# Input squares taken as tiles land, later blocks' squares from token rows, and input scalings placed later in the passage

## The chip, the cores and the metric

The kernel runs on one core of a Trainium2 chip. The metric is the device time of one execution in microseconds (us). The engines are PE (TensorE, the matrix engine; PEld is its loading of weights), DVE (VectorE), ACT (ScalarE), POOL (GpSimd) and SP (SyncE, which here only issues DMAs). Each engine runs its own instructions in the order in which they were placed, and waits on semaphores for what other engines or DMAs deliver.

## The reference, cut to what matters

The reference is one inference step of a two-layer decoder trunk. Layer 0 is a Mamba-2 mixer and a SwiGLU feed-forward, layer 1 a sliding-window attention and a SwiGLU feed-forward. Of it, the change touches only the first step, the RMS norm of the input ahead of the mixer's input projection:

```
def _rmsnorm(x, g):
    xf = x.astype(jnp.float32)
    r = lax.rsqrt(jnp.mean(xf * xf, axis=-1, keepdims=True) + EPS)
    return (xf * r).astype(x.dtype) * g

zxbcdt = _rmsnorm(h, p['ssm_norm_g'][i]) @ w_in
...
dt_raw = zxbcdt[..., D_INNER + CONV_DIM:]
```

There are 64 sampled tokens, 16 meta tokens and 1024 prompt tokens, 1104 in all, each with 1024 features.

## The kernel before, in words

The 1104 tokens are worked on in two halves, of 592 and 512 tokens. A half's tokens lie in SBUF turned: features on the 128 partitions, as 8 tiles (`k`, KD = 8) of one column per token. A product in float32 precision is made of three matmuls on high and low parts: `uH` and `uL` of the activations, `wH` and `wL` of the weights. The high part is a cast on ACT, the low part a subtraction on DVE or POOL (`_split_high`, `_split_low`, `split_copy`).

Because the tokens stand on columns, their squares are summed over partitions by matmuls whose weights are a tile of squares (one block of up to 128 tokens) and whose moving operand is one column of ones. The mean goes from PSUM into `v` (DVE), the root is a power of -0.5 on POOL, and to scale columns the roots `r` are put on a diagonal (`dg`, DVE) and spread over all partitions by a matmul with ones. The first half has five blocks: three in its first part (336 tokens, `As`) and two in its second part (256 tokens, `Bs`).

`input_first` (the first 46 us) has an order written out by hand for PE, DVE, ACT and POOL (`in_order` adds dependencies between an engine's instructions in the order in which they were traced). It loads the tokens as two arrays, warms PE up with matmuls on ones, squares the first part two tiles at a time, sums, makes the roots, then scales and splits tile by tile and multiplies with the first two weight tiles (`dense`). In between it squares the second part on ACT and POOL, sums it on PE ahead of tile 6, and splits the low part of the weights on POOL. Then it scales and multiplies the second part. After it comes the convolution of the two finished products (`conv`, whose copies of `cstate` run on POOL), and the projection of dt.

`input_second` is the same norm for the second half, 512 tokens in four blocks. It is a generator whose steps `boundary` (the passage from the first half to the second) interleaves with the end of the first half by a string of letters: `x`, `s` and `b` are its steps (squares; sums, roots and diagonals; spread, scalings and splits), `l` the late gate of the last head group, `n`, `r`, `y` the steps of that group's norm, each `o` one product of the group before with `w_out`, each `w` one product of the last group. This string fixes the order of PE alone. A product accumulates in one of two accumulators (`acc`), which DVE frees by adding it to the residual (line 921).

All other order is that of a planner, which places instructions by its own simulated clock and by priorities (`ahead` raises them). It also orders the DMAs on SP's queue. Weights come through a ring of two raw tiles (`ws`), two high and two low tiles, and each split pair is also stored to DRAM (`kept`) for the second half.

Of the kernel before, what the change touches and what calls it, by code (L numbers as in the profile page):

```python
# [14 lines left out]
AF = mybir.ActivationFunctionType  # L15
ALU = mybir.AluOpType
# [4 lines left out]
D = 1024  # L21
KD = 8
# [4 lines left out]
EPS = 1e-5  # L27
# [67 lines left out]
class Weights:  # L95
# [67 lines left out]
    def load(self):  # L163
        for s in self.queue[: max(NWS - 1, 1)]:
            self._load(s)
# [82 lines left out]
class Mamba:  # L248
# [51 lines left out]
    def input_first(self):  # L300
# [7 lines left out]
        for q, k in ((nc.sync, 0), (nc.scalar, 4), (nc.sync, 2), (nc.scalar, 6)):  # L308
            load(q, 0, slice(k, k + 2))
        W._load(W.queue[0])  # L310
        load_vectors(K, I, self.hp)
        K.load_ident()
        W._load(W.queue[1])
        for k in (0, 4):
            load(nc.sync, 1, slice(k, k + 4))
        self.wdt = self.kp.tile([128, KD, 32], F32, name="wdt")
# [19 lines left out]
        def square(i, k, eng):  # L336
            d, src = sq[k // 4][:, k % 4 : k % 4 + 2, at[i]], h[:, k : k + 2, at[i]]
            if eng is nc.scalar:
                eng.activation(d, src, AF.Square)
            else:  # L340
                eng.tensor_tensor(d, src, src, ALU.mult)

        def sums(i, cs, order):
            ps = {c: self.ps() for c in cs}
            for x, k in enumerate(order):
                for c in cs:
                    o, n = blocks[c]
                    src = sq[k // 4][:, k % 4, o : o + n]
                    nc.tensor.matmul(ps[c][:n, 0:1], src, one[:, 0:1], start=x == 0, stop=x == KD - 1)
            return ps  # L350

        def means(ps, cs):
            for c in ps:
                n = blocks[c][1]
                nc.vector.tensor_scalar(v[:n, c : c + 1], ps[c][:n, 0:1], 1.0 / D, EPS, ALU.mult, ALU.add)
            nc.gpsimd.tensor_tensor(r[:, cs], v[:, cs], e[:, cs], ALU.pow)
# [32 lines left out]
        warm(5)  # L389
        for k, eng in ((0, nc.scalar), (4, nc.vector), (2, nc.scalar), (6, nc.vector)):  # L390
            square(0, k, eng)
        pa = sums(0, As, (0, 1, 4, 5, 2, 3, 6, 7))
        means(pa, A)
# [5 lines left out]
        W._split_low(W.queue[0], nc.gpsimd)  # L399
        scaled(0, 0, ra)  # L400
        for k in range(KD):
            high(0, k)
            if k + 1 < KD:
                scaled(0, k + 1, ra)
            low(0, k)
            if k in (4, 5):
                square(1, 2 * (k - 4), nc.scalar)
                square(1, 2 * (k - 4) + 4, nc.gpsimd)
            if k == 6:
                pb = sums(1, Bs, (0, 1, 4, 5, 2, 3, 6, 7))  # L410
                means(pb, B)
                W._split_low(W.queue[1], nc.gpsimd)
            for t in range(2):
                dense(t, 0, k, 0, self.uH, start=k == 0)
                dense(t, 0, k, 0, self.uL)
        diagonal(Bs)
        for t in range(2):
            for k in range(KD):
                dense(t, 0, k, 1, self.uH, stop=k == KD - 1)
            if t == 0:  # L420
                rb = spread(1, Bs)
                scaled(1, 0, rb)
        for k in range(KD):
            high(1, k)
            if k + 1 < KD:
                scaled(1, k + 1, rb)
            low(1, k)
            for t in range(2):
                dense(t, 1, k, 0, self.uH, start=k == 0)
                dense(t, 1, k, 0, self.uL)  # L430
                dense(t, 1, k, 1, self.uH, stop=k == KD - 1)
        for _ in range(2):
            W.queue.pop(0)
# [8 lines left out]
    def input_second(self):  # L442
# [6 lines left out]
        pair = [sq[:, 2 * i : 2 * i + 2, :n] for i in range(2)]  # L449
        for i in range(4):  # L450
            nc.scalar.activation(pair[i > 0], h[:, 2 * i : 2 * i + 2], AF.Square)
            if i:
                nc.gpsimd.tensor_tensor(pair[0], pair[0], pair[1], ALU.add)
        nc.gpsimd.tensor_tensor(sq[:, 0, :n], sq[:, 0, :n], sq[:, 1, :n], ALU.add)
        yield
        ps = self.ps()
        for c, (o, m) in enumerate(H["blocks"]):
            nc.tensor.matmul(ps[:m, 2 * c : 2 * c + 1], sq[:, 0, o : o + m], K.ones[:, 0:1], start=True, stop=True)
        v = self.small([128, 4], "xv")
        nc.vector.tensor_scalar(v[:], ps[:, :8].rearrange("p (c two) -> p c two", two=2)[:, :, 0], 1.0 / D, EPS, ALU.mult, ALU.add)  # L460
# [530 lines left out]
    def boundary(self, inp, G2, G):  # L991
# [6 lines left out]
        part = dict(x=inp, s=inp, b=inp, l=late, n=nrm, r=nrm, y=nrm, o=self.out(G2, 0), w=self.out(G, 0, True))  # L998
        for x in "xloosonoboorooywwwwwwww":
            next(part[x])  # L1000
# [38 lines left out]
    def run(self):  # L1039
        tc, nc, K, I, O = self.tc, self.nc, self.K, self.I, self.O  # L1040
        with ExitStack() as st:
# [16 lines left out]
            for hf in range(2):  # L1058
# [5 lines left out]
                if hf == 0:  # L1064
                    K.scratch = big[:, :4096]
                    self.input_first()
                    xbc = self.xbc(hf, 0, range(6))
                    next(xbc)
                    self.dt_proj(hf)
# [1598 lines left out]
def tokens(inputs):  # L2668
# [3 lines left out]
    return {"tokens_a": turned(x[:cut]), "tokens_b": turned(x[cut:end]), "tokens_c": turned(x[end:])}  # L2672
# [25 lines left out]
```

## Time and profile before

| | us |
|---|---|
| median of 3 runs | 2812.53 (2809.44 to 2813.52) |
| the profiled execution's own time | 2812.34 |
| its span in the trace | 2810.5 |
| PE busy | 2737.9 (97% of the span) |
| DVE busy | 1988.0 (71%) |
| ACT busy | 1196.4 (43%) |
| POOL busy | 541.6 (19%) |

Times in the profile are microseconds from the span's start. A row of the view of instructions in order of time gives the start, the duration, the engine, the line of the kernel, the operation, what it writes and reads, how many instructions were merged, and in brackets how long the engine had been idle before it and what ended that. A row of a view of stretches gives the stretch, its length, the busy time and number of instructions of each engine, the clock that TensorE was granted (1.00 is full), the DMA engines' busy share and GB/s. SPq, POOLq and so on are an engine's sequencer, which issues DMAs and waits.

### The profile page before, as it was taken

The page shows a single profiled execution, that of the slowest core. Times are in us where ns is not written, and L with a number is a line of the kernel's source. Part 1 is how long each engine was busy: PE and PEld are TensorE (multiplying, and loading weights), DVE is VectorE, ACT ScalarE, POOL GpSimd, SP SyncE. Part 2 cuts the span into 40 slices and gives each one's busy share as a digit, 9 for nine tenths or more (in the row PEclk, how much of TensorE's full clock was granted, in tenths as well). Part 3 has the DMA queues.
Part 4 walks back from the last instruction along what each step waited for, and adds up shares of the span by engine and source line. Part 5 has one row for each costly group of instructions (what it writes and reads, how often), then busy time and mean ns, then how long its engine had stood idle before and what let it go on. Part 6 is the DMA issues. An engine that isn't in the chain of part 4 may idle for free. (4 is left out here: it accounts for less than half of the span.)

```text
span 2810.5 us, 50267 instructions
## 1 busy us (share of the span) xinstructions
PE 2737.9 (97%) x19693; PEld 2532.9 (90%) x19693; DVE 1988.0 (71%) x3398; ACT 1196.4 (43%) x2483; POOL 541.6 (19%) x749
## 2 busy tenths in 40 slices
PE   8999999899999999999999999999999999999998
PEld 7888999887887799999999997767999999999998
DVE  5778666557574698787779791455479877877886
ACT  3666554347442244343343243456334433434224
POOL 2475545415233100000000002343220000000000
PEclk8999999999999899999999999999999999999999
DMA  6776766466554434344378662011714443447764
GB/s 218 242 241 203 268 224 232 174 235 208 198 179 163 146 101 175 123 161 142 127 262 310 240 211 90 23 30 36 225 59 140 157 141 125 164 141 285 276 219 160
DMA packets 260849, 495.45 MB, mean 176 GB/s; under 512 B 23556, under 2 KB 139908, under 8 KB 260612
## 3 DMA queue, kind: packets, MB, share of 16 engines
q1 hardware_dynamic: 256612, 485.00, 50.3%
q10 hardware_dynamic: 4000, 7.24, 0.7%
q8 instruction: 155, 2.54, 0.4%
q14 instruction: 82, 0.67, 0.1%
HBM read 316.87 MB, written 175.30 MB: 175 GB/s over the span
## 5 line engine op out<-in xcount | busy, mean ns | idle before, releaser
L1246 ACT CAST wo<-ws 128x512 fp32r<-128x512 f32 x428 | 264.5, 622 | 538.2 <-PE wacc L1591 250.9
L1590 PE MATMUL dacc<-bo,wo 128*128 128x276 f32 (+1 forms) x1232 | 355.6, 289 | 4.4 <-ACT sumX L1778 2.1
L1591 PE MATMUL dacc<-bo,wo 128*128 128x276 f32 (+1 forms) x1232 | 356.1, 289 | 0.0
L1592 PE MATMUL dacc<-bo,wo 128*128 128x276 f32 (+1 forms) x1232 | 354.9, 288 | 0.0
L1247 DVE TENSOR_TENSOR wo<-ws,wo 128x512 fp32r<-128x512 f32 x428 | 296.4, 697 | 55.4 <-ACT wo L1246 42.1
L75 PE MATMUL acc<-uH,wH 128*128 128x336 f32 (+2 forms) x808 | 269.0, 333 | 3.9 <-ACT wH L138 3.5
L77 PE MATMUL acc<-uH,wL 128*128 128x336 f32 (+2 forms) x808 | 267.7, 331 | 0.6 <-DVE wL L149 0.6
L76 PE MATMUL acc<-uL,wH 128*128 128x336 f32 (+2 forms) x808 | 268.2, 332 | 0.0
L1590 PEld LDWEIGHTS dacc<-bo,wo 128*128 128x128 f32 x1232 | 232.8, 189 | 5.2 <-ACT sumX L1778 2.3
L1591 PEld LDWEIGHTS dacc<-bo,wo 128*128 128x128 f32 x1232 | 231.8, 188 | 0.0
L1592 PEld LDWEIGHTS dacc<-bo,wo 128*128 128x128 f32 x1232 | 231.8, 188 | 0.0
L75 PEld LDWEIGHTS acc<-uH,wH 128*128 128x128 f32 x808 | 155.1, 192 | 20.3 <-issue 6.1
L76 PEld LDWEIGHTS acc<-uL,wH 128*128 128x128 f32 x808 | 154.9, 192 | 12.8 <-issue 4.1
L77 PEld LDWEIGHTS acc<-uH,wL 128*128 128x128 f32 x808 | 154.5, 191 | 12.8 <-issue 3.1
L668 DVE SCALAR_TENSOR_TENSOR cc<-raw,vectors_sb,cc 128x616 f32<-128x616 f32 (+1 forms) x144 | 133.9, 937 | 41.9 <-ACT cc L666 40.2
L2443 POOL MEMSET mask<- 128x64 f32 x1 | 0.2, 152 | 715.5 <-PE dacc L1592 715.5
L75 PE MATMUL acc<-yH,wH 128*128 128x336 f32 (+1 forms) x360 | 123.4, 343 | 5.8 <-DVE hA L921 3.0
L76 PE MATMUL acc<-yL,wH 128*128 128x336 f32 (+1 forms) x360 | 121.3, 337 | 0.5 <-DVE yL L82 0.5
L77 PE MATMUL acc<-yH,wL 128*128 128x336 f32 (+1 forms) x360 | 121.4, 337 | 0.2 <-DMA wL<-kept 0.2
L1766 DVE TENSOR_TENSOR hN<-hN,dacc 128x552 f32<-128x552 f32 (+1 forms) x132 | 95.0, 723 | 20.6 <-PE dacc L1592 19.9
L1590 PE MATMUL wacc<-B11H,wo 128*128 128x276 f32 (+1 forms) x352 | 105.4, 299 | 3.5 <-DVE big L921 3.5
L1590 PE MATMUL wacc<-N4H,wo 128*128 128x276 f32 (+1 forms) x352 | 102.3, 291 | 4.4 <-DVE hA L1603 1.9
(569 smaller groups left out, 8562.2 us busy)
## 6 DMA issues: line engine op xcount, KB each, us to landing
kept<-wH SPq DMA_DIRECT2D x56, 512.0 KB, 3.1
kept<-wL SPq DMA_DIRECT2D x56, 512.0 KB, 3.0
ws<-ffn_w_gate SPq DMA_DIRECT2D x44, 512.0 KB, 4.2
ws<-ffn_w_up SPq DMA_DIRECT2D x44, 512.0 KB, 4.9
ws<-ffn_w_down SPq DMA_DIRECT2D x44, 512.0 KB, 6.1
ws<-ssm_w_in SPq DMA_DIRECT2D x40, 512.0 KB, 6.5
wH<-kept SPq DMA_DIRECT2D x38, 512.0 KB, 3.4
wL<-kept SPq DMA_DIRECT2D x38, 512.0 KB, 4.3
```

The costliest lines, as they stand in the source:

```text
L75: nc.tensor.matmul(out, wH, xH, start=start, stop=False)
L76: nc.tensor.matmul(out, wH, xL, start=False, stop=False)
L77: nc.tensor.matmul(out, wL, xH, start=False, stop=stop)
L668: nc.vector.scalar_tensor_tensor(o, raw[:, k : k + n], w(k), o, ALU.mult, ALU.add)
L1246: nc.scalar.copy(H, src)
L1247: (low or nc.vector).tensor_tensor(L, src, H.bitcast(F32), ALU.subtract)
L1590: nc.tensor.matmul(out, wH, xH, start=start, stop=False, skip_group_check=True)
L1591: nc.tensor.matmul(out, wH, xL, start=False, stop=False, skip_group_check=True)
L1592: nc.tensor.matmul(out, wL, xH, start=False, stop=stop, skip_group_check=True)
L1766: add = lambda d, s: nc.vector.tensor_tensor(d, d, s, ALU.add)
L2443: nc.gpsimd.memset(A.mask0[:, :NS], NEG)
```

## The change

In `input_first`, one token load moves from ACT's queue to SP's, the second weight tile is loaded ahead of the small vectors, and two loads of token rows (tokens on partitions, 128x1024 each) are added into the tiles `rows`. Warm-up is three matmuls instead of five. The first part's squares are made one tile at a time, on ACT and DVE in turn, and each is summed at once. The later two blocks' squares are two ACT instructions on the rows with an accumulated sum per partition, which is a sum per token, so their matmuls leave PE. Scaling runs two tiles ahead instead of one. The low parts of the two weight tiles are split on DVE behind the first part instead of on POOL. The first convolution block's POOL instructions are ordered behind the last root. In `input_second`, the squares also come from four row loads, with accumulated sums on ACT; the additions on POOL and the sums on PE go. In `boundary`, the step with spread, scalings and splits stands behind two of the last group's products, and the norm's first two steps each stand one product earlier.

```diff
--- before.py
+++ after.py
@@ -305,14 +305,17 @@
         x = [I["tokens_a"], I["tokens_b"]]
         at = [slice(0, cut), slice(cut, H["n"])]
         load = lambda q, i, ks: q.dma_start(h[:, ks, at[i]], x[i][:, ks])
-        for q, k in ((nc.sync, 0), (nc.scalar, 4), (nc.sync, 2), (nc.scalar, 6)):
+        for q, k in ((nc.sync, 0), (nc.scalar, 4), (nc.sync, 2), (nc.sync, 6)):
             load(q, 0, slice(k, k + 2))
-        W._load(W.queue[0])
+        for w in W.queue[:2]:
+            W._load(w)
         load_vectors(K, I, self.hp)
         K.load_ident()
-        W._load(W.queue[1])
         for k in (0, 4):
             load(nc.sync, 1, slice(k, k + 4))
+        rows = [self.quad("xr") for _ in range(2)]
+        for i in range(2):
+            nc.sync.dma_start(rows[i][:], I["token_rows"][i])
         self.wdt = self.kp.tile([128, KD, 32], F32, name="wdt")
         nc.sync.dma_start(self.wdt[:].rearrange("p k m -> p (k m)"), I["ssm_w_in"][40, :, :256])
         load_params(K, I, self.kp)
@@ -333,26 +336,23 @@
             for _ in range(n):
                 nc.tensor.matmul(idle[:], one[:, :128], one[:, :512], start=True, stop=True)
 
-        def square(i, k, eng):
-            d, src = sq[k // 4][:, k % 4 : k % 4 + 2, at[i]], h[:, k : k + 2, at[i]]
-            if eng is nc.scalar:
-                eng.activation(d, src, AF.Square)
-            else:
-                eng.tensor_tensor(d, src, src, ALU.mult)
-
-        def sums(i, cs, order):
+        def sums(cs):
             ps = {c: self.ps() for c in cs}
-            for x, k in enumerate(order):
+            for x, (k, eng) in enumerate(product((0, 4, 2, 6), (nc.scalar, nc.vector))):
+                k += eng is nc.vector
+                d, src = tile(k, 0), h[:, k, at[0]]
+                if eng is nc.scalar:
+                    eng.activation(d, src, AF.Square)
+                else:
+                    eng.tensor_tensor(d, src, src, ALU.mult)
                 for c in cs:
                     o, n = blocks[c]
-                    src = sq[k // 4][:, k % 4, o : o + n]
-                    nc.tensor.matmul(ps[c][:n, 0:1], src, one[:, 0:1], start=x == 0, stop=x == KD - 1)
-            return ps
-
-        def means(ps, cs):
-            for c in ps:
+                    nc.tensor.matmul(ps[c][:n, 0:1], tile(k, 0)[:, o : o + n], one[:, 0:1], start=x == 0, stop=x == KD - 1)
+            for c in cs:
                 n = blocks[c][1]
                 nc.vector.tensor_scalar(v[:n, c : c + 1], ps[c][:n, 0:1], 1.0 / D, EPS, ALU.mult, ALU.add)
+
+        def roots(cs):
             nc.gpsimd.tensor_tensor(r[:, cs], v[:, cs], e[:, cs], ALU.pow)
 
         def diagonal(cs):
@@ -386,49 +386,50 @@
 
         A, B = slice(0, 3), slice(3, 5)
         As, Bs = range(0, 3), range(3, 5)
-        warm(5)
-        for k, eng in ((0, nc.scalar), (4, nc.vector), (2, nc.scalar), (6, nc.vector)):
-            square(0, k, eng)
-        pa = sums(0, As, (0, 1, 4, 5, 2, 3, 6, 7))
-        means(pa, A)
+        warm(3)
+        sums(As)
+        roots(A)
         diagonal(As)
         warm(1)
         ra = spread(0, As)
         for t in range(2):
             ws[t] = W._split_high(W.queue[t])
-        W._split_low(W.queue[0], nc.gpsimd)
-        scaled(0, 0, ra)
+        for k in range(2):
+            scaled(0, k, ra)
         for k in range(KD):
             high(0, k)
-            if k + 1 < KD:
-                scaled(0, k + 1, ra)
+            if k in (2, 4):
+                c = 2 + k // 2
+                nc.scalar.activation(rows[c - 3][:], rows[c - 3][:], AF.Square, accum_out=v[:, c : c + 1])
+            if k + 2 < KD:
+                scaled(0, k + 2, ra)
             low(0, k)
-            if k in (4, 5):
-                square(1, 2 * (k - 4), nc.scalar)
-                square(1, 2 * (k - 4) + 4, nc.gpsimd)
-            if k == 6:
-                pb = sums(1, Bs, (0, 1, 4, 5, 2, 3, 6, 7))
-                means(pb, B)
-                W._split_low(W.queue[1], nc.gpsimd)
+            if k == 5:
+                nc.vector.tensor_scalar(v[:, B], v[:, B], 1.0 / D, EPS, ALU.mult, ALU.add)
+                roots(B)
             for t in range(2):
                 dense(t, 0, k, 0, self.uH, start=k == 0)
                 dense(t, 0, k, 0, self.uL)
+        W._split_low(W.queue[0], nc.vector)
         diagonal(Bs)
+        W._split_low(W.queue[1], nc.vector)
         for t in range(2):
             for k in range(KD):
                 dense(t, 0, k, 1, self.uH, stop=k == KD - 1)
             if t == 0:
                 rb = spread(1, Bs)
-                scaled(1, 0, rb)
+                for k in range(2):
+                    scaled(1, k, rb)
         for k in range(KD):
             high(1, k)
-            if k + 1 < KD:
-                scaled(1, k + 1, rb)
+            if k + 2 < KD:
+                scaled(1, k + 2, rb)
             low(1, k)
             for t in range(2):
                 dense(t, 1, k, 0, self.uH, start=k == 0)
                 dense(t, 1, k, 0, self.uL)
                 dense(t, 1, k, 1, self.uH, stop=k == KD - 1)
+        self.rooted = [x for x in traced[begin:] if x.engine == nc.gpsimd.engine]
         for _ in range(2):
             W.queue.pop(0)
         place_params(K)
@@ -446,18 +447,13 @@
         for k in range(0, KD, 2):
             nc.sync.dma_start(h[:, k : k + 2], self.I["tokens_c"][:, k : k + 2])
         sq = self.gp.tile([128, 4, 592], F32, name="sq", tag="xT", bufs=3)
-        pair = [sq[:, 2 * i : 2 * i + 2, :n] for i in range(2)]
-        for i in range(4):
-            nc.scalar.activation(pair[i > 0], h[:, 2 * i : 2 * i + 2], AF.Square)
-            if i:
-                nc.gpsimd.tensor_tensor(pair[0], pair[0], pair[1], ALU.add)
-        nc.gpsimd.tensor_tensor(sq[:, 0, :n], sq[:, 0, :n], sq[:, 1, :n], ALU.add)
-        yield
-        ps = self.ps()
-        for c, (o, m) in enumerate(H["blocks"]):
-            nc.tensor.matmul(ps[:m, 2 * c : 2 * c + 1], sq[:, 0, o : o + m], K.ones[:, 0:1], start=True, stop=True)
         v = self.small([128, 4], "xv")
-        nc.vector.tensor_scalar(v[:], ps[:, :8].rearrange("p (c two) -> p c two", two=2)[:, :, 0], 1.0 / D, EPS, ALU.mult, ALU.add)
+        nc.gpsimd.memset(v[:], 0.0)
+        for c in range(nb):
+            row = sq.rearrange("p a b -> p (a b)")[:, 1024 * (c % 2) : 1024 * (c % 2) + 1024]
+            nc.sync.dma_start(row, self.I["token_rows"][2 + c])
+            nc.scalar.activation(row, row, AF.Square, accum_out=v[:, c : c + 1])
+        nc.vector.tensor_scalar(v[:], v[:], 1.0 / D, EPS, ALU.mult, ALU.add)
         r = rsqrt(nc, self.wk, v[:], nb, "rx")
         self.rtok = [r[:, i : i + 1] for i in range(nb)]
         both = self.quad("rb")
@@ -995,8 +991,8 @@
         traced = self.nc.cur_bb.bb.instructions
         start = len(traced)
         inp, late, nrm = (self.ahead(x) for x in (inp, self.gate_late(G), self.norm(G, 3)))
-        part = dict(x=inp, s=inp, b=inp, l=late, n=nrm, r=nrm, y=nrm, o=self.out(G2, 0), w=self.out(G, 0, True))
-        for x in "xloosonoboorooywwwwwwww":
+        part = dict(x=inp, b=inp, l=late, n=nrm, r=nrm, y=nrm, o=self.out(G2, 0), w=self.out(G, 0, True))
+        for x in "xloonoooroooywwbwwwwww":
             next(part[x])
         for x in part.values():
             for _ in x:
@@ -1064,8 +1060,11 @@
                 if hf == 0:
                     K.scratch = big[:, :4096]
                     self.input_first()
+                    traced = nc.cur_bb.bb.instructions
+                    begin = len(traced)
                     xbc = self.xbc(hf, 0, range(6))
                     next(xbc)
+                    in_order(tc, self.rooted[-1:] + traced[begin:], nc.gpsimd)
                     self.dt_proj(hf)
                 else:
 
@@ -2669,7 +2668,8 @@
     x = np.concatenate([np.asarray(inputs[n]).reshape(-1, D) for n in ("x_sample", "meta_tokens", "x_prompt")])
     cut, end = HALVES[0]["split"][1:]
     turned = lambda a: np.ascontiguousarray(a.reshape(-1, KD, 128).transpose(2, 1, 0))
-    return {"tokens_a": turned(x[:cut]), "tokens_b": turned(x[cut:end]), "tokens_c": turned(x[end:])}
+    rows = np.ascontiguousarray(x[cut:].reshape(6, 128, D))
+    return {"token_rows": rows, "tokens_a": turned(x[:cut]), "tokens_b": turned(x[cut:end]), "tokens_c": turned(x[end:])}
 
 
 def device_shape(n, shape):
```

## The prediction

> **What bounds the kernel now.** I read the page's first lines, then the busy time of the engines by stage, then who waited for whom in the two stages that the change touches, and there the instructions in order of time.
>
> ```profile
> span 2810.5 us, 50267 instructions
> ...
> PE 2737.9 (97%) x19693; PEld 2532.9 (90%) x19693; DVE 1988.0 (71%) x3398; ACT 1196.4 (43%) x2483; POOL 541.6 (19%) x749
> ```
>
> PE, the matmul engine, is busy for 97% of the span. Work on another engine costs nothing until PE waits for it; a microsecond less of PE's waiting, or of PE work at half clock, ends everything behind it earlier. PE's two longest waits between 480 and 600 us (in total, times, longest):
>
> ```profile
> PE ps L458 <- POOL sq L454: 6.1, 1, 6.1
> PE acc L75 <- DVE hA L921: 2.6, 1, 2.6
> ```
>
> Both lie in the passage between the two halves of the sequence, which the diff touches. The other place that it touches is the first 46 us. Both stages also lose to a second thing, PE's clock. The input stage by stretches (columns: length, then busy time of PE, PEld, DVE, ACT and POOL, granted clock, DMA):
>
> ```profile
> 8.84:13.50 4.66, 4.66 (x49) 4.66 (x48) 0.29 (x3) 1.57 (x2) 0.00 (x0) 1.00 1.00 301
> 13.50:21.80 8.30, 3.58 (x10) 1.79 (x9) 4.91 (x8) 0.52 (x2) 5.78 (x7) 0.55 1.00 326
> 21.80:28.40 6.60, 6.59 (x24) 6.34 (x25) 5.86 (x13) 4.13 (x9) 0.00 (x0) 0.53 0.55 218
> 28.40:32.60 4.20, 4.20 (x35) 4.20 (x34) 0.16 (x1) 0.00 (x0) 0.00 (x0) 0.86 0.00 0
> 32.60:39.40 6.80, 6.80 (x30) 6.72 (x30) 4.09 (x7) 0.54 (x2) 3.98 (x4) 0.59 0.32 105
> 39.40:45.70 6.30, 6.22 (x49) 5.82 (x48) 5.35 (x16) 3.23 (x9) 0.00 (x0) 1.00 0.13 53
> ```
>
> The reader sees the sums of squares of the first three blocks (4.66 us), 8.3 us in which the roots are made and spread, the first part's products at half clock, 4.2 us of sums for the later two blocks that interrupt them, and 6.8 us again at little over half clock behind those sums.
>
> **Input stage, up to the first product.** What stands between the sums' end and the products, on DVE and on POOL (GpSimd):
>
> ```profile
> 13.33 0.52 DVE L355 TENSOR_SCALAR xv<-ps 80x1 f32<-80x1 f32 x3 [4.37 <-PE ps L349]
> 16.15 3.58 DVE L361 TENSOR_SCALAR dg<-cmask_sb,xr 80x80 f32<-80x80 f32 x3 [2.30 <-POOL xr L356]
> ```
> ```profile
> 14.81 0.40 POOL L650 COPY raw<-cstate 128x24 f32<-128x24 f32 x2 [13.51 <-DMA cstate<-state_conv]
> 15.26 0.85 POOL L356 TENSOR_TENSOR xr<-xv,xe 128x3 f32<-128x3 f32 x1
> 16.08 2.51 POOL L149 TENSOR_TENSOR wL<-ws,wH 128x512 fp32r<-128x512 f32 x2
> ```
>
> The means are ready at 13.85 (13.33 + 0.52), but POOL takes its queue in order and has two convolution copies ahead of the root, which wait for a DMA until 14.81: the root starts 1.4 us late. Then the three diagonals take 3.58 us, 1.19 each, while POOL splits weights. The same operation in the passage, with POOL free, is this row, 0.22 each:
>
> ```profile
> 510.75 0.88 DVE L466 TENSOR_SCALAR rb<-cmask_sb,rx_y 128x128 f32<-128x128 f32 x4 [1.13 <-POOL rx_y L91]
> ```
>
> The change takes the split and the squares off POOL and orders the first block's copy behind the last root. So three diagonals cost 0.7 instead of 3.58 (2.9 less), and the root starts with the means (1.4 less). From the sums' end to the first product there remain 0.35 for the means, 0.95 for the root, 0.75 for the diagonals and then what it is now from the last diagonal (16.15 + 3.58 = 19.73) to the first product at 21.8, 2.1: 4.1 us instead of 8.3.
>
> When do the sums end? Now ten warm-up instructions run from 1.45 to 9.0, and the sums stand behind them on PE, with squares that were ready earlier:
>
> ```profile
> 1.45 7.55 PE L334 MATMUL ps<-one 128*128 128x512 f32 x10 [1.45 <-DVE one L326]
> ```
> ```profile
> 8.09 0.86 DVE L341 TENSOR_TENSOR sq<-hA 128x672 f32<-128x672 f32 x1 [2.07 <-DMA hA<-tokens_a]
> ```
> ```profile
> 6.74 0.33 PEld L334 LDWEIGHTS ps<-one 128*128 128x128 f32 x1 [0.52 <-issue]
> ```
>
> Six warm-up instructions instead of ten end where now the seventh's weights load, about 6.6. The last token tile lands at 8.09 through ACT's queue; as third tile on SP it lands then at the latest, having fewer bytes ahead of it. Its two squares, each half of such an instruction on two engines, end by 8.6 and leave a quarter of the sums, 1.2 us, so PE is the limit: 6.6 + 4.66 = 11.3 at full clock, against 13.5. The first product then starts at 11.3 + 4.1 = 15.4 instead of 21.8. What moved on SP: one tile of 336 KB onto it, the second weight tile ahead of the small loads, and two row loads of 512 KB ahead of the parameters. At the stretch's 326 GB/s the rows delay everything behind them, the convolution state first, by 1.05 MB / 326 = 3.2 us; only the copies of L650 wait for that, after the change behind the roots.
>
> **Input stage, from the first product on.** Now 23.9 us (21.8 to 45.7). The sums of the later blocks leave PE: 4.2 us. Their squares become two ACT instructions over rows with an accumulated sum. Such a square of 128x1024 is in the passage's rows, and the reading of the accumulator in the attention's:
>
> ```profile
> L451 ACT ACTIVATE sq<-big x4: 1043/1054/1065, 486.1 to 497.1; 128x1024 f32<-128x1024 f32 x4
> ```
> ```profile
> L2226 ACT ACTIVATION_READ_ACCUMULATOR work<-work x128: 186/190/201, 1774.0 to 1976.2; 128x1 f32 x128
> ```
>
> That is 1.25 each, 2.5 on an ACT that is busy for 4.13 of 6.60; behind each the next conversion is up to 1 us late, and since scaling now runs two tiles ahead the products lose at most that once, 0.7. The two weight splits move to DVE at 1.23 each:
>
> ```profile
> 46.34 1.23 DVE L149 TENSOR_TENSOR wL<-ws,wH 128x1024 fp32r<-128x1024 f32 x1 [1.45 <-ACT wH L138]
> ```
>
> They lie behind the first part's last low part, so PE waits there for the first split, and the second part's scaling stands behind the second. Step by step from the first product, taken as 0: DVE has finished the eight low parts at 7.5 (the 5.86 us in which it now does six, extended to eight, less its start 1.1 ahead, with the two late conversions); first split 8.75; two diagonals 9.25; second split 10.5; scaling of the second part from 10.5. From there to the end of the stage it is 7.4 now:
>
> ```profile
> 38.30 0.87 DVE L372 SCALAR_TENSOR_TENSOR sq<-hA,vectors_sb,ps 128x256 f32<-128x256 f32 x2 [1.82 <-PE ps L368]
> ```
>
> (38.30 to 45.7). Sum 17.9 instead of 23.9. The stage ends at 15.4 + 17.9 = 33.3 instead of 45.7: **12.4 us**. If the sums run at half clock it is 7.7 (below).
>
> **Passage.** PE by stretches, the last row the whole (length, busy, clock, DMA):
>
> ```profile
> 501.40:507.50 6.10, 0.07 (x1) 0.86 0.82 267
> 507.50:509.30 1.80, 1.75 (x9) 0.50 1.02 419
> 509.30:512.60 3.30, 3.30 (x14) 0.50 0.18 73
> 526.00:530.60 4.60, 1.48 (x12) 0.91 0.48 191
> 530.60:536.60 6.00, 6.00 (x24) 0.50 0.53 175
> 494.70:566.90 72.20, 62.46 (x422) 0.91 0.50 177
> ```
>
> Of 72.2 us PE idles 9.7 (72.20 - 62.46); the sums that leave cost 1.75; 3.3 and 6.0 us of products run at half clock, 4.65 too much. At most 9.7 + 1.75 + 4.65 = 16.1 are to be had. Why PE waits at 501.4, on POOL:
>
> ```profile
> 503.84 2.43 POOL L854 TENSOR_TENSOR sq<-sq,th 128x592 f32<-128x592 f32 x1
> 506.24 1.26 POOL L454 TENSOR_TENSOR sq<-sq 128x512 f32<-128x512 f32 x1
> ```
>
> This last addition of input squares and the three before it (L453) go; POOL keeps the gate's (L854) and two roots. What is late next is L854's sum for the norm, which now stands third on PE: its square ends at 499.91 (row below), plus up to 2.43: 502.3, so PE waits 0 to 1 us.
>
> ```profile
> 499.21 0.70 ACT L853 ACTIVATE th<-xT 128x592 f32<-128x592 f32 x1 [1.00 <-DVE xT L847]
> ```
>
> The second stall has this cause on DVE:
>
> ```profile
> 520.25 4.42 DVE L475 SCALAR_TENSOR_TENSOR sq<-big,vectors_sb,rb 128x512 f32<-128x512 f32 x4 [0.80 <-ACT rb L471]
> 524.60 1.28 DVE L82 TENSOR_TENSOR uL<-sq,uH 128x512 fp32r<-128x512 f32 x2
> 525.80 0.76 DVE L921 TENSOR_TENSOR hA<-hA,acc 128x592 f32<-128x592 f32 x1
> ```
>
> The scalings hold DVE for 4.4 us and the product's adding, which frees an accumulator for PE, comes behind. The change puts them two products into the last eight, away from the norm's spread (which also takes an accumulator). The burst stays: with two accumulators and 3.3 us a product, an adding may be late by 3.3 - 0.8 = 2.5, so 4.4 costs 1.9. I take off 1 for POOL, 0.5 for the accumulator under the norm's spread, 2 for the burst and 1.5 for what half clock they bring: 5. Saving **11 us**; ends 16.1 and, if the burst costs what the second stall and its half clock cost now (3.1 + 3.0), 6. Four row loads, 2.1 MB on SP, take no PE time (DMA share 0.50 over the passage); the squares' work on ACT is as before plus 4 x 0.19.
>
> **Sum.** 12.4 + 11 = 23.4 against the profiled execution's 2812.34 (span 2810.5 plus 1.84 around it; 0.2 below the median of 2812.53): 2789. Behind both stages PE is fed by queues that follow its consumption, so I pass the gain on whole. The order elsewhere is a planner's, which sees other times: 4 us either way, an estimate: one or two waits of the size of the second above (2.6).
>
> **Rivals.**
> *Half clock in the sums.* Clock 0.50 stretched sums to 1.87 us for 8 instructions (0.23 each), against 4.66 for 48 at 1.00 (0.10):
>
> ```profile
> 507.55 1.87 PE L458 MATMUL ps<-cmask_sb,sq 128*128 128x1 f32 x8 [6.08 <-POOL sq L454]
> ```
>
> Of the ten warm-up instructions the first six took 5.3 us (1.45 to 6.74, 0.88 each) and the last four 2.3 (0.57 each): the clock rose among the four that go. If it has not risen behind six, one-column sums will not raise it (28.40 to 32.60 lost it), and they take 9.3: 4.7 more, **2794**. The Trainium skill (TensorE: Matmul & The Clock Gate, "Part 1: The HAM clock gate") says that a free-running window of about 3.4 us decides, wherever the first matmul falls in it. By that rule six instructions suffice in some executions only; the rises and falls in these stretches agree with it.
>
> *A copy still in front of the root.* The diff orders only what the first convolution block issues. If the second's copy is placed ahead of the first root, this waits for the state until 14.81 + 3.2 = 18.0, 18.4 with the copy, instead of 11.7: 6.7 more, **2796**. For it: both copies stood there. Against it: the load comes later, the root earlier.
>
> *The passage gives half back.* The burst costs 6 instead of about 2, and 1 more at the norm: **2794**. The Trainium skill (Advanced Engine Details and Errata, "VectorE Performance Modes") says that GpSimd shares VectorE's second port. That speaks against the move, since the last products' squares are added on POOL beside it. The 1.19 against 0.22 of the diagonals agrees.
>
> *Slower.* SP issues in order, and the row loads of the passage need a buffer that the norm frees only at 486.05:
>
> ```profile
> 485.28 0.77 DVE L82 TENSOR_TENSOR yL<-xT,yH 128x592 fp32r<-128x592 f32 x1
> ```
> ```profile
> 455.99 1.99 SPq L447 DMA_DIRECT2D big<-tokens_c  x4
> 460.92 0.45 SPq L608 DMA_DIRECT2D eo<-acsd  x1
> ```
>
> If they are queued straight behind the tokens (457.98), ahead of the decay and weight loads from 460.92 on, those wait until 486, 28 us from the tokens' end, and then for the rows themselves, 2.1 MB at 326 GB/s or 6.4 us: up to 34 us of starved PE, 2789 + 34 = **2823**. It decides from a hold of 29 us on. Against it: SP now goes from the tokens straight to the decay loads, and a planner that knows the buffer is taken has no cause to put a blocked load between.
>
> **How the numbers follow.** Forecast 2789: 0.47; half clock 0.22; the copy 0.12; the passage 0.09; the slower one 0.05; 0.05 for several together that end within 0.2% (5.6 us, about what a measurement of this kernel can tell from no change). Low end: 16.1 instead of 11, and the planner's 4: 2780. High end: half clock and a passage of 6 with the planner's 4: 2803. Faster 0.90, same 0.05, slower 0.05.
>
> **What would show it.** First product near 15.4 and end of the stage near 33; diagonals of 0.22 each; no copy ahead of POOL's first root; no PE sums between the products; in the passage no wait for POOL over 1 us and one for DVE of about 2 beside the scalings. Wrong if the sums take 9 us, if SP stands still before 486, or if PE's waits elsewhere grow by more than 4.

## The result, and the profile after

| us | before | after |
|---|---|---|
| median of 5 runs each, same chip | 2809.44 (2806.05 to 2813.52) | 2795.93 (2792.01 to 2798.55) |
| ratio | | 0.9948, 95% interval 0.9932 to 0.9964 |
| span of the profiled execution | 2810.5 | 2796.7 |

The changed kernel is 13.5 us faster by the medians and 13.8 by the profiled spans, where 23.4 were forecast. (The forecast time, 2789, was counted from 2812.34; the kernel before came out 3.1 lower here than in its first three runs, by the medians.) The second table follows PE through both traces; the last column is how far the changed kernel is ahead there.

| us from the span's start | before | after | ahead |
|---|---|---|---|
| first product | 21.8 | 17.1 | 4.7 |
| end of the input stage | 45.7 | 34.6 | 11.1 |
| start of the passage | 494.7 | 486.4 | 8.3 |
| end of the passage | 566.9 | 551.6 | 15.3 |
| end of the span | 2810.5 | 2796.7 | 13.8 |

So the terms are 11.1 for the input stage (forecast 12.4), 2.8 lost ahead of the passage (forecast 0, with 4 either way), 7.0 for the passage (forecast 11), and 1.5 lost behind it (forecast 0). They are read from one execution of each kernel; how far they repeat is said with each below.

The input stage of the changed kernel in stretches (length; busy time of PE, PEld, DVE, ACT and POOL; clock; DMA). The first row holds the sums, the second runs to the first product:

```profile
6.73:12.60 5.87, 5.87 (x50) 5.87 (x48) 0.82 (x3) 2.58 (x3) 0.00 (x0) 0.87 1.06 388
12.60:17.10 4.50, 3.29 (x9) 1.79 (x9) 1.90 (x7) 0.49 (x2) 0.85 (x1) 0.50 1.00 344
```

The sums, 48 of the 50 matmuls in the first row, take 5.9 us instead of 4.66, at a clock that falls on the way. Behind them the chain is as forecast; last mean, roots and diagonals in order of time:

```profile
12.73 0.16 DVE L353 TENSOR_SCALAR xv<-ps 128x1 f32<-128x1 f32 x1 [0.27 <-PE ps L350]
```
```profile
13.04 0.85 POOL L356 TENSOR_TENSOR xr<-xv,xe 128x3 f32<-128x3 f32 x1 [11.79 <-DVE xv L353]
22.63 2.38 POOL L356 TENSOR_TENSOR xr<-xv,xe 128x2 f32<-128x2 f32 x1 [8.73 <-DMA big<-state_ssm]
```
```profile
13.93 0.65 DVE L361 TENSOR_SCALAR dg<-cmask_sb,xr 80x80 f32<-80x80 f32 x3 [1.04 <-POOL xr L356]
```

The first root starts 0.15 us behind the last mean (12.73 + 0.16), no copy is ahead of it, and three diagonals take 0.65 instead of 3.58. The second root takes 2.38, where it took 0.90 in the kernel before (start 32.99), and the later blocks' diagonals wait 0.60 for it on DVE.

In the passage PE's waits (in total, times, longest) and the clock around the longest single one:

```profile
PE acc L75 <- DVE hA L917: 3.4, 3, 1.8
PE acc L75 <- DVE zT L837: 2.1, 1, 2.1
PE acc L76 <- DVE yL L82: 0.5, 1, 0.5
```
```profile
486.40:489.80 3.40, 3.40 (x26) 1.00 1.01 396
489.80:492.00 2.20, 0.07 (x2) 1.00 0.51 207
492.00:497.00 5.00, 5.00 (x24) 0.66 0.71 256
486.40:551.60 65.20, 58.92 (x414) 0.97 0.58 210
```

The 6.1 us for POOL are gone, the wait for DVE's adding (L917 here, L921 before; line numbers move with each edit) is 3.4 where it was 2.6, and a new wait of 2.1 for `zT` stands at 489.8 with half clock behind it. `zT` is late because of ACT. SP's queue, ACT and DVE there:

```profile
477.74 1.21 SPq L454 DMA_DIRECT2D sq<-token_rows  x2
...
482.75 0.33 SPq L454 DMA_DIRECT2D sq<-token_rows  x1
```
```profile
481.57 1.06 ACT L455 ACTIVATE sq<-sq 128x1024 f32<-128x1024 f32 x1
...
488.45 1.06 ACT L455 ACTIVATE sq<-sq 128x1024 f32<-128x1024 f32 x1 [2.92 <-DMA sq<-token_rows]
...
489.50 1.03 ACT L138 CAST wH<-ws 128x1024 fp32r<-128x1024 f32 x1
490.44 0.65 ACT L836 ACTIVATE zT<-acc 128x592 f32<-128x592 f32 x1
```
```profile
491.12 0.77 DVE L837 SCALAR_TENSOR_TENSOR zT<-zT,acc 128x592 f32<-128x592 f32 x1 [7.33 <-ACT zT L836]
```

The four row loads share two buffers. The third can be issued only when the first square has been taken (481.57 + 1.06 = 482.63), and lands 5.7 us later, while the DMA engines are busy throughout (1.01). ACT takes its queue in order, so a weight cast and the gate's `tanh`, which need no rows, stand 2.92 us behind a square that does.

The sizes are those of one execution. Seven traces have this passage unedited (the first, and those below in which only the input stage differs or nothing does). In them ACT waits 1.5 to 3.1 for the third row and PE 0.6 to 2.3 for `zT`; the wait for the adding is 3.2 to 3.5; and in six of the seven, not in this one, PE also waits 1.6 for POOL at the norm. The passage takes 64.8 to 66.9, so it saves 5.3 to 7.4.

### The profile page after: what moved, and what is told of

Same layout as the page of the kernel before. It is cut to its first block, busy times and chain, and to the rows that moved or that the text cites. A ratio compares the mean times of both kernels' runs of the same rounds, so it can differ in the third digit from the quotient of the medians.

```text
span 2796.7 us, 50176 instructions
## 1 busy us (share of the span) xinstructions
PE 2723.8 (97%) x19649; PEld 2515.4 (90%) x19649; DVE 1988.1 (71%) x3401; ACT 1193.6 (43%) x2491; POOL 525.2 (19%) x740
## 4 chain that ended last, share of the span: by engine, by line
PE 84%; DVE 8%; ACT 2%; DMA 2%; issue 1%; POOL 1%; SPq 0%; POOLq 0%; DVEq 0%; ACTq 0%
PE wacc L1589 10%; PE wacc L1591 10%; PE wacc L1590 10%; PE acc L75 6%; PE acc L76 6%; PE acc L77 6%; PE dacc L1589 5%; PE dacc L1590 5%; PE dacc L1591 5%; PE pP L75 2%; PE pP L76 2%; PE pP L77 2%; PE ps L746 1%; PE ps L749 1%; DVE cc L664 1%
```

## The experiments

**The two stages by themselves.** Each kernel keeps one stage of the change and takes the other from before. For the input stage alone (`input_second` and the string of `boundary` go back; the string is shown):

```diff
-        for x in "xloonoooroooywwbwwwwww":
+        for x in "xloosonoboorooywwwwwwww":
```

> Only the input stage is changed; input_second and the order of the passage are those of before. Theory A (the two stages gain apart, and what one gains passes on to the end but for the planner's order in between): the stage ends near 34.6 us as in the changed kernel (45.7 before), the passage takes its 72 us from the first product with w_out to the projection of dt, and the whole is 13.5 - 7.0 = 6.5 us faster than before, ratio 0.9977. Rival B (the time that the input stage gains is lost again behind it, and the whole gain of 13.5 us is the passage's): ratio within 0.9990 to 1.0010, with PE's waits between 46 and 480 us grown by some 10 us.

Measured: 2799.72, ratio 0.9970 (0.9959 to 0.9981); stage end at 34.5, passage 72.4 us.

For the passage alone, `input_first` and the POOL order go back (this line of it is shown, as a difference from the changed kernel):

```diff
-                    in_order(tc, self.rooted[-1:] + traced[begin:], nc.gpsimd)
```

> Only the passage is changed; the input stage is that of before. Theory A: the input stage ends at 45.7, the passage takes about 65 us instead of 72.2, and the whole is some 7 us faster, ratio 0.9975; the ratios of this and of the input stage alone multiply to that of the whole change, 0.995. Rival B: 13 us faster here, 0.9953.

Measured: 2804.41, ratio 0.9982 (0.9970 to 0.9995); passage 494.6 to 561.1, 66.4 us. By the medians the input stage alone gives 9.1 us and the passage alone 4.4, where 6.5 and 7 were expected; both expected ratios lie inside the intervals. The product of both ratios is 0.9952, against 0.9948 for the whole change: within their intervals the two parts add up, and no dependence of one on the other shows.

**POOL beside DVE.** The two weight splits go back to POOL, one beside the diagonals of each part (the first is shown):

```diff
+        W._split_low(W.queue[0], nc.gpsimd)
         for k in range(2):
             scaled(0, k, ra)
```

> The changed kernel with the low parts of the first two weight tiles split on POOL again, at their old places: one beside the diagonals of the first part, one beside those of the second. Theory A (POOL slows DVE's diagonals): the three diagonals take 3.6 us instead of 0.65 and the first product starts 2.9 us later, at 20.0; DVE is rid of 2 x 1.23 us behind the first part, so of the 2.9 about 1.2 come back, and the stage ends 1 to 3 us later than 34.6. Rival B (the diagonals of before were slow for another reason, not the split): they stay at 0.65 and the stage ends up to 1.2 us earlier.

Measured: ratio 0.9966 (0.9952 to 0.9980), first product at 18.9 and stage end at 36.4, both 1.8 later (20.0 and 1 to 3 later were expected).

```profile
13.82 2.51 POOL L149 TENSOR_TENSOR wL<-ws,wH 128x512 fp32r<-128x512 f32 x2
```
```profile
13.89 2.72 DVE L361 TENSOR_SCALAR dg<-cmask_sb,xr 80x80 f32<-80x80 f32 x3 [1.04 <-POOL xr L356]
```

The same three diagonals take 2.72 while POOL splits and 0.65 while it doesn't. So POOL's split slows the diagonals, as the forecast said. Of the 2.9 us that the forecast took off for them the split alone brings back 2.1; before, POOL went on with squares beside the third diagonal (18.55 to 20.63), which was not tried by itself.

**Why the sums were slow.** Five warm-ups as before, and one (each is two matmuls in the trace):

```diff
-        warm(3)
+        warm(5)
```

> The changed kernel with five warm-up matmuls again. In six executions with three or five so far the sums began between 5.5 and 8.8 us, and ended at 12.5 to 12.7 behind three, at 13.3 to 13.7 behind five. Theory A (the clock rises about 3.4 us into full work and falls about 3.4 us into the sums; three matmuls buy an earlier begin with a part of the sums at half clock): the sums begin at 8.4 to 8.9, run at full clock throughout, take 4.7 to 4.9 and end at 13.2 to 13.7, the first product at 17.6 to 18.2 instead of 17.1. Rival B (the sums end with the last token tile's squares, whatever the warm-up): they end at 12.6.

Measured, from the one profile: sums 8.18 to 13.0 at full clock, first product 17.43, 0.3 later than with three. That is Theory A's full clock throughout; begin, end and first product each lie some 0.2 ahead of the ranges expected.

```diff
-        warm(3)
+        warm(1)
```

> One warm-up of two matmuls instead of three of two ahead of the sums; all else as in the changed kernel. In seven traces so far the clock fell some 3.4 us after the sums had begun, and the sums of the three-warm-up kernels ended at 12.5 to 12.7 whenever they began. Theory A (the clock follows how dense PE's work was, and 128x1 sums count as little): two matmuls leave no dense stretch, the clock never rises ahead of the sums, and all 48 run at about 0.19 us each: from about 5.2, when the first squares are there, 9.3 us, end near 14.5, first product near 19. Theory B (the fall comes at a fixed time from the span's start): the sums end at 12.5 to 12.7 again. Theory C (the sums keep a clock that has risen, and the warm-up only delayed them): they end near 10, two thirds of a microsecond behind the last squares at about 7.4 or as fast as 0.10 each allows, first product near 14.5.

Measured, from the one profile (matmuls in order of time):

```profile
1.45 2.08 PE L337 MATMUL ps<-one 128*128 128x512 f32 x2 [1.45 <-DVE one L329]
5.28 9.12 PE L350 MATMUL ps<-one,sq 128*80 128x1 f32 x48 [1.75 <-ACT sq L345]
```

Theory A: 48 sums take 9.12 us, 0.19 each, end at 14.4, first product 18.83. The clock never rises on sums alone, though PE is busy without a gap. The expectation's "3.4 us after the sums had begun" was too coarse, though. What repeats is how long the full clock lasts. Sums in stretches of the changed kernel, then of the kernel with four row buffers (below), whose input stage is the same (PE's busy time and count, clock):

```profile
6.80:7.60 0.80, 0.80 (x6) 1.00 1.02 415
7.60:11.00 3.40, 3.40 (x36) 1.00 1.06 380
11.20:12.40 1.20, 1.20 (x8) 0.50 1.12 397
```
```profile
5.70:7.70 2.00, 2.00 (x23) 1.00 1.06 421
7.80:12.40 4.60, 4.60 (x26) 0.50 1.06 381
```

In the first the sums begin slowly, run at 0.09 each for 3.4 us and fall to half; in the second the fast stretch began during the warm-up and is over by 7.7. Counted in half-clock time the work is the same in both: 6 warm-up matmuls by 0.88 (1.45 to 6.73 holds six) and 48 sums by 0.19 are 14.4 us; one fast stretch of 3.4 saves 3.4, so the end is 1.45 + 14.4 - 3.4 = 12.45 wherever the stretch lies. The traces with three warm-ups end their sums at 12.45 to 12.7, though the sums begin anywhere from 5.54 to 6.73. This is what the Trainium skill (TensorE: Matmul & The Clock Gate, "Part 1: The HAM clock gate") describes as a free-running window of about 3.4 us; these traces agree, and add that in them a window full of one-column sums counts as idle. The column of the clock must be read with the durations beside it: in the run with one warm-up it says 1.00 for this stretch, at 0.19 a sum.

```profile
5.28:14.40 9.12, 9.12 (x49) 1.00 1.05 393
```

**The POOL order in the input stage.** The changed kernel without the line of `in_order` shown for the passage alone.

> The line that orders the first convolution block's POOL instructions behind the last root is taken out. Theory A (the two copies of the convolution state come between the two roots, and the state has landed by then): first root at 13.0 as in the changed kernel, second root at most 0.5 later than 22.6, first product 17.1 and stage end 34.6 to 35.1. Rival B (the copies come ahead of the first root, as in the kernel before, and wait for the state): first root at 18 or later, first product near 22, stage end near 40.

Measured, from the one profile: first product 17.03, stage end 34.4.

```profile
12.94 0.85 POOL L356 TENSOR_TENSOR xr<-xv,xe 128x3 f32<-128x3 f32 x1 [11.62 <-DVE xv L353]
17.15 0.78 POOL L646 COPY raw<-cstate 128x24 f32<-128x24 f32 x2 [3.35 <-DMA cstate<-state_conv]
22.53 2.38 POOL L356 TENSOR_TENSOR xr<-xv,xe 128x2 f32<-128x2 f32 x1 [4.60 <-ACT uH L375]
```

Theory A: the copies come between the roots, when POOL has nothing else to do. The line brings nothing in this trace; the rival of a copy ahead of the first root does not occur with or without it.

**The new wait in the passage.** Four row buffers instead of two:

```diff
-            row = sq.rearrange("p a b -> p (a b)")[:, 1024 * (c % 2) : 1024 * (c % 2) + 1024]
+            if c < 2:
+                row = sq.rearrange("p a b -> p (a b)")[:, 1024 * c : 1024 * c + 1024]
+            else:
+                row = self.quad("xr")[:]
```

> The changed kernel, but the passage's third and fourth token rows go into two buffers of their own, so that their loads do not wait for the squares of the first two. Theory A (the third square waits on ACT for its load, and holds up the conversion and the tanh behind it, which frees PE's accumulator): ACT's wait for the token rows (2.9 and 1.15 us) goes, PE's wait of 2.1 us for the last gate tile (line 837) goes with the half clock behind it (5 us at 0.66, 1.7 us too much), and the passage takes 61 to 62 us instead of 65.2: about 4 us faster than the changed kernel, 2792. Rival B (the loads land late because the DMA engines are full at that place, share 1.01): the third row still lands as late, the wait stays, and the time is that of the changed kernel, 2796 within 2.

Measured: 2790.14, ratio 0.9942 (0.9925 to 0.9959); the passage takes 64.1 us, where 61 to 62 were expected. ACT no longer waits for rows, but PE still waits 1.7 us for `zT`. DVE there:

```profile
483.49 4.18 DVE L465 TENSOR_SCALAR rb<-cmask_sb,rx_y 128x128 f32<-128x128 f32 x4 [1.13 <-POOL rx_y L91]
487.60 0.76 DVE L840 SCALAR_TENSOR_TENSOR zT<-zT,acc 128x592 f32<-128x592 f32 x1
```

The norm's diagonals came earlier, beside POOL's work, took 1.05 each where the prediction's row had 0.22, and `zT` stands behind them. The wait moved. So the next kernel also makes the diagonals on ACT:

```diff
-            nc.vector.tensor_scalar(dg[:, o : o + m], K.ident, r[:, c : c + 1], None, ALU.mult)
+            nc.scalar.activation(dg[:, o : o + m], K.ident, AF.Copy, scale=r[:, c : c + 1])
```

> As the version with four row buffers, and the four diagonals of the passage's input roots are made on ACT instead of DVE. In the four-row version ACT's wait for the rows was gone, but PE still waited 1.7 us for the last gate tile, whose adding stood on DVE behind the four diagonals: 4.18 us there, with POOL at work. Theory A (POOL beside DVE makes these diagonals slow, and they stand in the adding's way): with the diagonals on ACT (0.3 to 0.4 us each) PE's wait of 1.7 for the gate tile goes; the passage takes about 62 us from its first product to the projection of dt, about 2 less than with four rows alone; 2788. Rival B (the gate tile is late for another reason): the wait stays, time as with four rows, 2790.

Measured: 2790.30, ratio 0.9936 (0.9921 to 0.9951); PE's waits in the passage:

```profile
PE acc L75 <- DVE hA L920: 3.2, 2, 1.8
PE ps L881 <- POOL sq L853: 0.6, 1, 0.6
```

The wait for `zT` is gone, and the passage takes 63.0 us instead of 65.2. By their intervals this kernel and the changed one could not be told apart yet.

**The burst of scalings.** In the changed kernel the scalings lie beside POOL's additions of the next norm (L1158), and single instructions take up to 1.95 instead of 0.74:

```profile
528.86 3.93 DVE L471 SCALAR_TENSOR_TENSOR sq<-big,vectors_sb,rb 128x512 f32<-128x512 f32 x4
...
533.32 0.76 DVE L917 TENSOR_TENSOR hA<-hA,acc 128x592 f32<-128x592 f32 x1
...
535.20 0.74 DVE L471 SCALAR_TENSOR_TENSOR sq<-big,vectors_sb,rb 128x512 f32<-128x512 f32 x1
...
536.47 1.95 DVE L471 SCALAR_TENSOR_TENSOR sq<-big,vectors_sb,rb 128x512 f32<-128x512 f32 x1
538.34 0.76 DVE L917 TENSOR_TENSOR hA<-hA,acc 128x592 f32<-128x592 f32 x1
...
543.59 0.76 DVE L917 TENSOR_TENSOR hA<-hA,acc 128x592 f32<-128x592 f32 x1
```
```profile
528.36 1.89 POOL L1158 TENSOR_TENSOR tot<-tot,sqh 128x592 f32<-128x592 f32 x1 [4.79 <-ACT sqh L1155]
535.24 2.63 POOL L1158 TENSOR_TENSOR tot<-tot,sqh 128x592 f32<-128x592 f32 x1 [4.99 <-ACT sqh L1155]
```

The addings stand 5.0 and 5.3 us apart here (533.32, 538.34, 543.59), and a product takes 3.3. Is it the raised priority of the scalings that lets them pass the adding? The step without it:

```diff
-            next(part[x])
+            next(part[x] if x != "b" else second)
```

> The changed kernel, but the step with the scalings and splits of the passage is placed without the raised priority, so that the planner may put the last products' adding ahead of them on DVE. Theory A (the burst of scalings that stands ahead of the adding on DVE costs PE 3.4 us in three waits beside it): PE's waits for line 917 fall from 3.4 to under 1 us, 2 to 3 us faster than the changed kernel's 2796. Rival B (the adding is late because DVE as a whole is full there, POOL's additions stretching the scalings from 0.74 to 1.9 us, whatever the order): the waits stay at 3 us or more, or move to the first projection after the passage.

Measured: 2794.97, ratio 0.9947 (0.9932 to 0.9962); PE waits for L917 3.4 in three waits, four scalings 3.95, one 1.95, as before the edit, and DVE's order there is the same. Priority is not the cause.

Then the place: on top of the diagonals on ACT, the step stands ahead of POOL's additions:

```diff
-        for x in "xloonoooroooywwbwwwwww":
+        for x in "xloonobooroooywwwwwwww":
```

> As the version with four rows and diagonals on ACT, with the scalings behind the third product of the passage, ahead of the norm's spread, instead of behind two of the last eight. Theory A (what the scalings cost PE comes from POOL's additions of the last products' squares beside them: with POOL at rest a scaling takes 0.74 and a burst of four 3.0, little over the 2.5 that an adding may be late): no scaling over 1.0 us, PE's waits for the adding under 1.5 in total instead of 3.4, the passage about 60 us, 2 faster than the version before. Rival B (the scalings cost PE the same wherever they stand, or delay the norm's four scalings and so the last products): waits of 3 us or more, at line 917's adding or for yH or yL.

Measured: 2796.11, ratio 0.9942 (0.9925 to 0.9959); the passage takes 60.8 us instead of 63.0. The first four scalings (L474 here) take 2.74 instead of 3.95, yet PE's waits for the adding stay at 3.0, in one wait:

```profile
501.49 0.77 DVE L920 TENSOR_TENSOR hA<-hA,acc 128x592 f32<-128x592 f32 x1
502.17 1.10 DVE L82 TENSOR_TENSOR uL<-sq,uH 128x512 fp32r<-128x512 f32 x1
503.20 2.42 DVE L474 SCALAR_TENSOR_TENSOR sq<-big,vectors_sb,rb 128x512 f32<-128x512 f32 x2
505.54 0.68 DVE L82 TENSOR_TENSOR uL<-sq,uH 128x512 fp32r<-128x512 f32 x1
506.14 0.74 DVE L474 SCALAR_TENSOR_TENSOR sq<-big,vectors_sb,rb 128x512 f32<-128x512 f32 x1
506.80 0.76 DVE L920 TENSOR_TENSOR hA<-hA,acc 128x592 f32<-128x592 f32 x1
```
```profile
501.42 2.98 POOL L149 TENSOR_TENSOR wL<-ws,wH 128x512 fp32r<-128x512 f32 x2 [6.75 <-ACT wH L138]
```

Between two addings stand scalings and their low parts, 4.6 us (502.17 to 506.80) against a product of 3.3. POOL was not at rest, as the expectation had it: it splits weights from 501.42 to 504.40, and beside that a low part takes 1.10 instead of 0.68 and two scalings 2.42 instead of 1.4 (half of the 2.74 for four). An estimate from these rows: about half of the 3.0 us of waiting is POOL's, and the other half comes from how many scalings and low parts are placed between two addings. No run has tried either by itself. The shorter passage did not show in the total.

**Changed kernel and best version side by side.** Both again, on one chip.

> The changed kernel again, beside the next one on the same chip: ratio to before 0.9948 give or take 0.0016, as it was measured first. Where its single executions differ, the first product is at 17.0 to 17.4 and the passage takes 64 to 67 us in whichever is profiled; more than that would mean that the account of the stages is one of a single execution.

Measured: 2795.86, ratio 0.9956 (0.9941 to 0.9972). Stage end at 34.6; the passage takes 66.5 us. Beside the wait for `zT` stands one that the first profile had not:

```profile
PE acc L75 <- DVE zT L837: 2.3, 1, 2.3
PE ps L878 <- POOL sq L850: 1.6, 1, 1.6
```

> The kernel with four row buffers and the passage's diagonals on ACT again, to tell it from the changed kernel with more runs. Theory A (the 2.2 us of the passage that it saved in its profile reach the end): 2 to 5 us faster than the changed kernel of this call, ratio to before 0.9930 to 0.9942. Rival B (the planner's order and the clock behind the passage give it back): within 1 us of the changed kernel, ratio 0.9945 to 0.9952.

Measured: 2786.50, ratio 0.9935 (0.9918 to 0.9953). Between these two kernels the means of 6 and 11 runs differ by 7.6 us, with a 95% interval of 3.0 to 12.2 worked out from their spread; the medians by 9.4. With four row buffers and the diagonals on ACT the kernel is faster than the changed one, by more than the 2 to 5 expected if the point value holds. The two profiles differ by 3.7 in span: 1.9 in the passage (66.5 to 64.6) and 1.6 on the way to it, where both have the same code. So only the 1.9 can be laid to the edit by these traces; the rest is not placed.

## Why the prediction was right or wrong, point by point

That the kernel gets faster, and that both stages give, was right, and 2795.93 lies between the 2780 and 2803 of the range. The point was 7 us too fast. Every term that missed by more than 1 missed towards too much gain; the time is inside the range because its upper end had room for half clock, a poor passage and the planner together, and a part of each came. The terms one by one:

- *End of the sums, 11.3.* They ended at about 12.6. The step "PE is the limit: 6.6 + 4.66 at full clock" failed. The rival of half clock had the cause but took it as all or nothing; the traces shown have one fast stretch of 3.4 us each, and in all with three warm-ups the sums end within 0.25 us of each other, as if it were always worth the same. Cost 1.3.
- *From the sums to the first product, 4.1.* It took 4.5, with root and diagonals as forecast.
- *From the first product to the stage's end, 17.9.* It took 17.5 (17.1 to 34.6). The second part's scaling began 9.9 us behind the first product (27.03), where 10.5 was worked out, and from there to the end it took 7.6 instead of 7.4. The later blocks' squares are 1.05 and 0.18 on ACT, by their rows, as the 1.25 assumed. What the row squares, the scaling two tiles ahead and the moved load each gave was not tried apart.
- *The gain passed on whole between the stages.* In the profile 2.8 were lost between 34.6 and 486.4. Two of PE's waits grew there by 2.9 in sum:

```profile
PE ps L811 <- DVE decs L781: 3.9, 1, 3.9
...
PE ps L811 <- POOL decB L784: 1.8, 1, 1.8
```

  Before they were 2.1 and 0.7. The same kernel's second profile has the same two waits and yet lost 1.6 less, PE being busy 1.3 us less. Over the twelve traces with the changed input stage, as it is or edited, this stretch takes 1.7 less to 3.9 more than the 449.0 of before, in the middle 0.7 more: the gain was passed on nearly whole, as forecast, and most of the 2.8 is one execution's.
- *Passage, 11.* It was 7.0. Of the 9.7 us in which PE idled, 3.5 were to remain: 1 for POOL, 0.5, and 2 for the burst. 6.3 remained (65.20 - 58.92): the burst cost 3.4, and 2.1 stood at a place that the prediction had not looked at. For the burst it counted one set of four scalings; the rows show scalings and low parts between several addings in a row, 4.3 and 4.6 us of them (534.00 to 538.34, 539.02 to 543.59) in the time of a product of 3.3. It costed the four row loads as "no PE time" and the squares "as before" on ACT by their work, and did not ask what stands behind ACT's wait for the third load. These two are the steps that failed. PE's busy time fell by 3.5 (62.46 to 58.92) instead of 4.9 (1.75 + 4.65 - 1.5); the new half clock at 492 to 497 (0.66 of 5.0 us) lost 1.7 where 1.5 was allowed for, and the other 1.2 are not accounted for.
- *POOL at the norm, 0 to 1.* None in the first profile, 1.6 in six of the seven traces of this passage: mechanism right, size too small, and the first profile is the exception.
- *SP held by the row loads (2823).* Did not occur: the loads stand at 477.74 to 484.97, and no wait for weights follows.
- *The passage gives half back (2794).* It did so in part: 4 of the 5 us by this profile, though only 1.4 of them by the burst. That GpSimd shares VectorE's second port (the Trainium skill, Advanced Engine Details and Errata, "VectorE Performance Modes") spoke against the move. The traces agree: the scalings beside POOL's additions took up to 1.95 for 0.74. The wait for the adding grew by 0.8 only, from 2.6 to 3.4.
- *Behind the passage, 0.* 1.5 lost, which no reading should be built on: two profiles of the same changed kernel end the passage at 551.6 and 551.3 and their spans at 2796.7 and 2787.5. This is also why the passage's 1 to 4 us in the experiments do not settle their totals.

## What to carry to other kernels

A new instruction on an in-order engine costs what stands behind it while it waits: ask of each transferred operand when its buffer comes free, when it lands, and which instruction of the critical path is next in that queue. Price an operation from a row in which the neighbours are busy as they will be, since a diagonal took 0.22 us with POOL at rest, and 0.91 or 1.05 with POOL at work beside it. When a stall is removed, look at what it hid: here the wait for rows, behind that the diagonals, and behind those nothing more for `zT`.

## What the runs showed of the hardware

- A stretch of one-column matmuls that keeps PE busy without a gap does not keep the clock: full speed lasted 3.4 us behind three warm-ups; behind five it held to the end of the sums (4.8 us at 0.10 a sum), and behind one it never came (0.19 a sum).
- The clock column read 1.00 over 9.12 us of sums at half speed in the run with one warm-up, so the durations decide.
- Two executions of one program differed by 9.2 us in span, 8.9 of it behind the passage (551 us). In the three stretches of 200 us from 1700 on the first shows 0.96, 0.98 and 0.99 of the clock, the second 0.98, 1.00 and 1.00. The middle one of each (length, PE's busy time and count, clock, DMA), first the first execution:

```profile
1900.00:2100.00 200.00, 188.70 (x1423) 0.98 0.35 101
```
```profile
1900.00:2100.00 200.00, 187.58 (x1434) 1.00 0.37 105
```
